# A fused hybrid layer on one core: two tiles that outlive the stages and hold what the next one reads first, a fourth quadrant sum formed with the others, memory keys transposed beside the pair products

## The chip, the core and the metric

One NeuronCore of one Trainium2 chip. The metric is the device time of one execution in microseconds, over several runs. TensorE multiplies matrices into PSUM, VectorE, ScalarE and GpSimd work on tiles in SBUF, and SyncE issues all the DMAs of this kernel in one queue, in program order: an issue that has to wait holds up all that stand behind it.

## What is computed

One layer over two groups of tokens: 1024 prompt tokens, and 8 requests of 16 new tokens each with a cache (128 "sample" tokens). The width is 1024, all numbers are fp32.

```python
u = layer_norm(x)                                   # both groups
q, k, v, g_a, x_r, g_b, q_m, g_c, g_m = split(u @ w_in)       # 1024 -> 11264
# A: differential attention, 8 heads; sample tokens also over cache_k, cache_v (512 past tokens)
o_a = diff_attn(q, k, v, cache) * silu(g_a)
# B: causal convolution of width 4, gated linear recurrence
o_b = rglru(conv(x_r)) * silu(g_b)
# C: attention into 256 memory tokens, 4 heads; sample tokens into cache_mem_k, cache_mem_v
mk, mv = split(mem_prompt @ w_mem_kv)               # mk, mv are outputs too
o_c = softmax(q_m @ mk.T / 16) @ mv * silu(g_c)
m = sum_i sigmoid(g_m[i]) * (o_i @ w_branch[i])
y = layer_norm(alpha * x + m @ w_o)
```

Further outputs are the new keys and values, the last recurrence state and the last rows before the convolution.

## The kernel before

**Products in split form.** TensorE multiplies in a reduced form of fp32 (fp32r). Each operand is split into an upper part, rounded by a ScalarE cast, and a lower part, the rest, by a VectorE subtraction (`split`, L135); `mm3` adds up three products: upper by upper, lower by upper, upper by lower. So the same names come in pairs: `uhi`, `ulo` (the activations, transposed, 1152 tokens), `xh`, `xl` (a weight tile from `xr`).

**Units.** Most of TensorE's work are units (`units_for`, L467): 24 products of 128x384 into a bank named `pj`, for one column tile of weights and one third of the tokens. `m_units` (L500) merges a branch: it loads a gate (`gmr`) and the sum so far (`mr`) from DRAM, adds the gated product and stores the sum (`d_m`). A stage is a `Window`: a list of small functions, `weave`d from its own steps and units that fill TensorE's time. A scheduler then places every instruction by priority, which follows program order but for hoists; tiles and banks carry the waits.

**Stages in order of time** (us of the profiled execution):

- to 196: norms, transposes, memory keys and values (stored in DRAM as `d_kv`), values
- to 683: prompt attention (`window_a`)
- to 720: `window_p` (L1100): `piece` loads quadrants of `u` (k halves by token halves) as `uq` and forms three sums and differences, split into `ut`; units for the merge gates fill
- to some 1335: `window_g` (L1167): the remaining projections in a two-by-two scheme with seven products instead of eight: 28 jobs of seven steps each (`step`, L1336), 24 products of 128x288 per half step into banks `ba`, `bb`, `bc`; the recurrence runs beside them. `start` (L1171) loads the fourth quadrant again (`uz`, ten loads), subtracts and writes the difference over the first part of `uhi`, `ulo`. `g_prep` (L1135) forms sums `s1`, `s2`, `s3` of weight quadrants
- to some 1545: `window_s` (L824): decode attention over the cache: `kload` (L853) brings keys of request b and head group g in two loads of 512 KB, TensorE transposes them (`ktr`), GpSimd puts the queries (`qz<-sq`) and new keys (`kT<-sk`) in place
- to some 1651: `window_c` (L726): memory attention of the prompt. `setup` loads the memory keys, `mk_tr` (L739) transposes them, four steps of four transposes, `qget` and `qput` load and scale and split the queries of a head
- to some 1750: `window_x` (L989): memory attention of the sample tokens, eight requests in turn; `load` (L1007) brings 1 MB of keys and 1 MB of values each; `xq` is the query, scaled by GpSimd from `xqr`
- to the end: the merge of the third branch, the output product, the last norm.

At the end of `window_s` and `window_x`, `swap` (L523) loads the next branch's output (`ocr`, twelve pieces through four buffers) and splits it over `uhi`, `ulo`.

## Time and profile before

| | |
|---|---|
| runs | 1966.18, 1965.82, 1960.79 us |
| median | 1965.82 us |
| profiled execution | 1961.36 us, span 1959.6 us |
| granted TensorE clock, mean | 0.996 |
| busy share TensorE, VectorE, ScalarE, GpSimd | 98%, 64%, 45%, 5% |
| moved by DMA | 296 MB, mean 151 GB/s |
| chain that ended last | TensorE 81%, DMA 8%, VectorE 5%, ScalarE 4% |

The profile shows one execution. Times in its rows count from the start of the span. A row of the timeline is one instruction or several merged ones; the bracket at its end gives how long the engine stood idle before it, and the work of which engine, line or DMA ended that. Products are pipelined: a row's length is longer than the distance to the next row's start, and it is the distance that counts in a series.

### The profile page before, as it was taken

The page shows a single profiled execution, that of the slowest core. Times are in us where ns is not written, and L with a number is a line of the kernel's source. Part 1 is how long each engine was busy: PE and PEld are TensorE (multiplying, and loading weights), DVE is VectorE, ACT ScalarE, POOL GpSimd, SP SyncE. Part 2 cuts the span into 40 slices and gives each one's busy share as a digit, 9 for nine tenths or more (in the row PEclk, how much of TensorE's full clock was granted, in tenths as well). Part 3 has the DMA queues.
Part 4 walks back from the last instruction along what each step waited for, and adds up shares of the span by engine and source line. Part 5 has one row for each costly group of instructions (what it writes and reads, how often), then busy time and mean ns, then how long its engine had stood idle before and what let it go on. Part 6 is the DMA issues. An engine that isn't in the chain of part 4 may idle for free.

```text
span 1959.6 us, 34499 instructions
## 1 busy us (share of the span) xinstructions
PE 1911.8 (98%) x13544; PEld 1811.2 (92%) x13544; DVE 1252.1 (64%) x2536; ACT 891.4 (45%) x1827; POOL 89.1 (5%) x174
## 2 busy tenths in 40 slices
PE   8999999999999999999999999998999999999998
PEld 8999999999999999999999999997788888789986
DVE  7731786677866667767666667664444675464397
ACT  5432565556655543334666666663333442231120
POOL 0000000000000000000000000000110001000000
PEclk9999999999999999999999999999999999999999
DMA  9753122212221174323444444458788875885332
GB/s 300 234 151 104 33 69 81 65 45 66 69 81 37 53 202 132 103 92 105 125 150 128 138 137 136 135 160 264 252 300 259 287 268 191 299 293 178 122 115 87
DMA packets 292114, 296.34 MB, mean 151 GB/s; under 512 B 17572, under 2 KB 249892, under 8 KB 291952
## 3 DMA queue, kind: packets, MB, share of 16 engines
q1 hardware_dynamic: 291952, 294.15, 47.0%
q8 instruction: 106, 1.74, 0.4%
q14 instruction: 56, 0.46, 0.1%
HBM read 209.01 MB, written 85.08 MB: 150 GB/s over the span
## 4 chain that ended last, share of the span: by engine, by line
PE 81%; DMA 8%; DVE 5%; ACT 4%; issue 2%; SPq 1%; DVEq 0%; ACTq 0%
PE pj L140 36%; PE ba L1359 9%; PE bb L1359 9%; PE bc L1359 9%; PE sc L140 5%; PE o L140 4%; PE tr L663 2%; PE tr L879 1%; PE pv L140 1%; PE tr L140 1%; DMA xk<-in_cache_mem_k_dram 1%; DMA ocr<-d_oT 1%; ACT K L589 1%; DVE w L258 1%; PE tr L1020 1%
## 5 line engine op out<-in xcount | busy, mean ns | idle before, releaser
L140 PE MATMUL pj<-uhi,xh 128*128 128x384 f32 x1248 | 428.4, 343 | 1.1 <-DVE gmr L513 1.1
L140 PE MATMUL pj<-uhi,xl 128*128 128x384 f32 x1248 | 421.9, 338 | 0.6 <-DVE xl L133 0.6
L140 PE MATMUL pj<-ulo,xh 128*128 128x384 f32 x1248 | 421.6, 338 | 0.0
L140 PEld LDWEIGHTS pj<-uhi,xh 128*128 128x128 f32 x1248 | 235.2, 188 | 5.4 <-issue 2.7
L140 PEld LDWEIGHTS pj<-uhi,xl 128*128 128x128 f32 x1248 | 234.9, 188 | 2.1 <-DVE xl L133 0.9
L140 PEld LDWEIGHTS pj<-ulo,xh 128*128 128x128 f32 x1248 | 235.3, 189 | 0.8 <-issue 0.4
L136 ACT CAST xh<-xr 128x512 fp32r<-128x512 f32 x143 | 85.5, 619 | 145.1 <-PE pj L140 100.1
L645 ACT ACTIVATE p<-p,sst 128x256 f32<-128x256 f32 (+6 forms) x128 | 100.6, 787 | 17.3 <-DVE sst L642 16.1
L140 PE MATMUL pj<-w,uhi 128*128 128x256 f32 x576 | 105.0, 282 | 0.5 <-ACT uhi L136 0.5
L140 PE MATMUL pj<-wo,mh 128*128 128x512 f32 x432 | 99.2, 390 | 0.6 <-ACT wo L136 0.3
L642 DVE CUSTOM_DVE_ANT_0 p<-sc,th 128x256 f32<-128x256 f32 (+6 forms) x128 | 96.4, 767 | 3.2 <-PE sc L140 2.0
L140 PEld LDWEIGHTS pj<-wo,mh 128*128 128x128 f32 x432 | 80.8, 188 | 18.9 <-ACT wo L136 1.6
L140 PE MATMUL sc<-K,Q 128*128 128x512 f32 (+4 forms) x384 | 94.6, 356 | 0.0
L513 DVE SCALAR_TENSOR_TENSOR gmr<-gmr,pj 128x384 f32<-128x384 f32 x72 | 39.7, 551 | 84.2 <-PE pj L140 61.6
L140 PEld LDWEIGHTS pj<-w,uhi 128*128 128x128 f32 x576 | 89.0, 189 | 1.3 <-ACT uhi L136 1.2
L133 DVE TENSOR_TENSOR xl<-xr,xh 128x512 fp32r<-128x512 f32 x104 | 70.6, 685 | 24.9 <-ACT xh L136 24.5
L140 PE MATMUL pj<-w,ulo 128*128 128x256 f32 x288 | 81.6, 284 | 1.7 <-DVE ulo L133 1.7
L140 PE MATMUL o<-v,wT 128*128 128x128 f32 x576 | 80.2, 278 | 0.0
L140 PEld LDWEIGHTS o<-v,wT 128*128 128x128 f32 x576 | 74.3, 192 | 3.4 <-ACT wT L169 1.5
L573 DVE SCALAR_TENSOR_TENSOR Q<-pj,Q 64x384 fp32r<-64x384 f32 (+1 forms) x48 | 24.5, 511 | 80.7 <-ACT Q L572 80.2
L589 ACT CAST K<-kr 64x384 fp32r<-64x384 f32 (+1 forms) x96 | 45.7, 476 | 48.4 <-DVE kr L584 47.3
L140 PEld LDWEIGHTS sc<-K,Q 128*128 128x128 f32 x384 | 63.9, 189 | 3.8 <-DVE sst L642 1.5
(323 smaller groups left out, 4284.1 us busy)
## 6 DMA issues: line engine op xcount, KB each, us to landing
xr<-in_w_in_dram SPq DMA_DIRECT2D x80, 512.0 KB, 4.0
ck<-in_cache_k_dram SPq DMA_DIRECT2D x32, 512.0 KB, 5.9
cv<-in_cache_v_dram SPq DMA_DIRECT2D x16, 1024.0 KB, 7.7
gmr<-d_gm SPq DMA_DIRECT2D x72, 192.0 KB, 5.2
xr<-in_w_branch_dram SPq DMA_DIRECT2D x24, 512.0 KB, 5.9
d_gm<-go SPq DMA_DIRECT2D x20, 576.0 KB, 3.2
d_m<-gmr SPq DMA_DIRECT2D x48, 192.0 KB, 3.1
mr<-d_m SPq DMA_DIRECT2D x48, 192.0 KB, 2.9
```

What stands on the lines that cost most here:

```text
L133: V.tensor_tensor(out, a, b, OP.subtract)
L136: SC.copy(hi, src)
L140: PE.matmul(out, a, b, start=start, stop=stop)
L258: V.tensor_tensor(l[:, 2 * j:2 * j + 2], src, raw(h[:, 2 * j:2 * j + 2]), OP.subtract)
L513: V.scalar_tensor_tensor(g, g, 1.0, t, op0=OP.add, op1=OP.mult)
L573: V.scalar_tensor_tensor(q[b], t[a, :n], -1.0, raw(q[a]), op0=OP.mult, op1=OP.subtract)
L589: SC.copy(kh[b], kr[a, :n])
L642: V.tensor_tensor_reduce(s[:, :L].rearrange("p (a b) -> p a b", a=nb), ps[z][:, :nb, :w], X["th"][:, 896 - 128 * i:896 - 128 * i + L].rear ...
L645: SC.activation(s[:, :L], s[:, :L], AF.Exp, scale=-1.0, bias=st_[:, z, i:i + 1], accum_out=st_[:, 2 + z, i:i + 1])
L663: PE.transpose(t[:, 128 * j:128 * j + 128], X["w", h, i][:, 128 * k:128 * k + 128], ident)
L879: PE.transpose(t[:, 128 * j:128 * j + 128], X["ck", n, s // 2][:, j, 128 * (s % 2):128 * (s % 2) + 128], ident)
L1359: PE.matmul(t, w[:, p, k, :], m[v][:, k, a], start=first and k == 0 and y == 0, stop=last and k == 3 and y == 2, skip_group_check=True)
```

## The change

- **Fourth quadrant.** `piece` in `window_p` forms the fourth difference from the quadrants that it has loaded anyway, into `uz` (a tile of the new pool `prek`, tag `pk`) and a small rest tile; `start` only splits it. The ten loads and their subtractions in `start` go.
- **Sums of weights.** `s1`, `s2`, `s3` live in a pool (`gs`) that is opened ahead of `window_p`; `g_prep(1)` is called at the end of `window_p`.
- **Two tiles that outlive the stages.** Tag `pk` of `prek` holds in turn `uz`, the first cache keys (`ck0`), the transposed memory keys (`mkr`) and the first keys of `window_x`. Tag `pq` of `preq` holds the first memory query (`qr`), then the first values of `window_x`.
- **Memory keys.** In `window_g`, beside jobs 1 to 5, `mk_get` loads a quarter of the keys and stores it to the output, `mk_tr` transposes it (four transposes), ScalarE copies, and a store takes it to DRAM (`d_mkT`). `c_get` at the end of `window_s` loads all of it, and the first query; `window_c` only splits.
- **Priority.** The last nine attention steps of `window_x` are placed with a priority higher by 100.
- The scratch area for dynamic DMA is set to 1024 bytes.

```diff
@@ window_c
-            mr = wk.tile([128, 2, D], F32, name="mr", tag="Gc")
+            X["qr"] = pre["q"]
             for j in range(4):
...
+                a = slice(2 * j, 2 * j + 2)
+                split(*[z[:, a] for z in X["mkT"]], pre["k"][:, a])
+                if j == 0:
+                    qput(0)
+            pre["xk"] = pre["p"].tile([128, 2, D], F32, name="xk", tag="pk")
+            pre["xv"] = pre["s"].tile([128, 2, D], F32, name="xv", tag="pq")
...
-        at = [lambda j=j: mk_tr(j) for j in range(4)]
+        at = []
         for h in range(MH):
+            if h == 3:
+                at.append(lambda: [SY.dma_start(pre["x" + z], A["cache_mem_" + z][0][0].rearrange(
+                    "(a p) h d -> p a (h d)", p=128)) for z in "kv"])
@@ window_s
+        def first_keys():
+            t = pre["p"].tile([128, 2, 4, 256], F32, name="ck0", tag="pk")
+            for e in range(2):
+                SY.dma_start(t[:, e], ck[0].rearrange("(a p) h d -> p a (h d)", p=128)[:, :, 256 * e:256 * e + 256])
+                X["ck", 0, e] = t[:, e]
...
+        def c_get():
+            pre["k"] = pre["p"].tile([128, 8, 256], F32, name="mkr", tag="pk")
+            SY.dma_start(pre["k"], d_mkT.rearrange("k p t -> p k t"))
+            pre["q"] = pre["s"].tile([128, 2, S], F32, name="qr", tag="pq")
+            SY.dma_start(pre["q"], d_qm[0:2, :, :S].rearrange("d p t -> p d t"))
@@ window_x
+            if b == 0:
+                X["k", 0], X["v", 0] = pre["xk"], pre["xv"]
                 return
...
+        def first(f):
+            with tc.high_priority(100):
+                f()
+        at[n:] = [lambda f=f: first(f) for f in at[n:]]
@@ window_p
+            sub(gp[1][c // 128], q[1, 1], q[0, 1])
@@ window_g
-            gp[0] = wk
-            g_prep(1)
             g_prep(2)
             for c, n in TCS:
-                t = wk.tile([128, 2, 4, 128], F32, name="uz", tag="go", bufs=2)[:, :, :, :n]
-                for k in range(2):
-                    SY.dma_start(t[:, k], d_u[4 * k:4 * k + 4, :, TH + c:TH + c + n].rearrange("k p t -> p k t"))
-                sub(t[:, 1], t[:, 1], t[:, 0])
                 a = (slice(None), slice(0, 4), slice(TH + c, TH + c + n))
-                split(uhi[a], ulo[a], t[:, 1])
+                split(uhi[a], ulo[a], gp[1][c // 128])
...
+        def mk_get(j):
+            c = slice(256 * j, 256 * j + 256)
+            mt_[j] = r = wk.tile([128, 2, 256], F32, name="mk", tag="mk", bufs=2)
+            SY.dma_start(r, d_kv[:, c].rearrange("(a p) d -> p a d", p=128))
+            SY.dma_start(A["out_4"][0, 0].rearrange("(a p) h d -> p a (h d)", p=128)[:, :, c], r)
+
+        def mk_tr(j):
...
+            o = wk.tile([128, 2, 256], F32, name="mo", tag="mo")
+            SC.copy(o, t.rearrange("p (a b) -> p a b", a=2))
+            SY.dma_start(d_mkT[2 * j:2 * j + 2].rearrange("k p t -> p k t"), o)
```

How the instructions stand. SyncE's queue where the memory attention goes over to its decode part (`d_oT` stores of the outputs, `d_m` stores and `gmr`, `mr` loads of the merge, `xqr` the decode query, `xG` its gate), before:

```order
L506 DMA gmr<-d_gm 128x384
L810 DMA d_oT_59<-oc 128x512 x4
L519 DMA d_m<-gmr 128x384
L509 DMA mr<-d_m 128x384
L997 DMA xqr<-d_qm 128x8x128
L1002 DMA xG<-d_gc 128x8x128
L1004 DMA xcs<-in_c_xsel_dram 128x64
L1012 DMA xk<-in_cache_mem_k_dram 128x2x1024
L1012 DMA xv<-in_cache_mem_v_dram 128x2x1024
```

and now:

```order
L805 DMA d_oT_59<-oc 128x512 x3
L520 DMA d_m<-gmr 128x384
L510 DMA mr<-d_m 128x384
L805 DMA d_oT_59<-oc 128x512
L453 DMA xr<-in_w_branch_dram 128x8x128
L507 DMA gmr<-d_gm 128x384
L1007 DMA xqr<-d_qm 128x8x128
L1012 DMA xG<-d_gc 128x8x128
L1014 DMA xcs<-in_c_xsel_dram 128x64
L1025 DMA xk<-in_cache_mem_k_dram 128x2x1024
```

The query stands directly behind a pair of merge transfers before; now a 512 KB weight load (`xr`) and a gate load stand between the last output store and it. The gate load takes a buffer that the store `d_m` ahead of it must have read.

TensorE where the memory attention's first scores (`sc`) are formed, before:

```order
L140 MATMUL pj<-uhi,xl 128x384
L140 MATMUL pj<-uhi,xh 128x384
L140 MATMUL pj<-ulo,xh 128x384
L140 MATMUL pj<-uhi,xl 128x384
L744 MATMUL tr<-ident,mr 128x128 x4
L140 MATMUL sc_17377<-mkT_17186,qm_17360 128x256
L140 MATMUL sc_17377<-mkT_17187,qm_17360 128x256
```

and now:

```order
L140 MATMUL pj<-uhi,xh 128x384
L140 MATMUL pj<-ulo,xh 128x384
L140 MATMUL pj<-uhi,xl 128x384
L140 MATMUL sc_17332<-mkT_17231,qm_17235 128x256
L140 MATMUL sc_17332<-mkT_17232,qm_17235 128x256
L140 MATMUL sc_17332<-mkT_17231,qm_17236 128x256
L140 MATMUL sc_17332<-mkT_17231,qm_17235 128x256
```

The transposes of the memory keys (`mr`) have gone from here. The scores stand behind the 24th product of the merge that is issued in this stage; before, behind the 72nd.

TensorE at the end of the decode part (`tr<-ident,xp` transposes the last probabilities, `pv` multiplies by the values, `o` sums the requests' parts), before:

```order
L140 MATMUL pj<-ulo,xh 128x384
L140 MATMUL pj<-uhi,xl 128x384
L1041 MATMUL tr<-ident,xp 128x128 x2
L140 MATMUL pv<-xv,xpT 32x256 x8
L140 MATMUL o<-xcs,xacc 128x64 x2
L140 MATMUL pj<-uhi,xh 128x384
L140 MATMUL pj<-ulo,xh 128x384
L140 MATMUL pj<-uhi,xl 128x384
```

and now:

```order
L140 MATMUL pj<-ulo,xh 128x384
L140 MATMUL pj<-uhi,xl 128x384
L140 MATMUL pv<-xv,xpT 32x256 x8
L140 MATMUL pj<-uhi,xh 128x384
L140 MATMUL pj<-ulo,xh 128x384
L140 MATMUL pj<-uhi,xl 128x384
L140 MATMUL o<-xcs,xacc 128x64 x2
L140 MATMUL pj<-uhi,xh 128x384
L140 MATMUL pj<-ulo,xh 128x384
```

The value products and outputs followed each other directly; now products of the merge stand between the transposes, the value products and the outputs. Behind the last output 1063 products of 128x384 remain, 1008 before.

## Rows read from the trace of the kernel before

**Rows 1.** The page, busy time by engine (busy us, share of the span, number of instructions):

```profile
PE 1911.8 (98%) x13544; PEld 1811.2 (92%) x13544; DVE 1252.1 (64%) x2536; ACT 891.4 (45%) x1827; POOL 89.1 (5%) x174
```

**Rows 2.** Stretches of the span: its bounds and length in us, busy time of each engine with its number of instructions, granted TensorE clock, mean busy share of the DMA engines, GB/s:

```profile
726.00:746.00 20.00, 15.69 (x109) 14.36 (x108) 13.19 (x24) 7.08 (x15) 0.00 (x0) 1.00 0.64 162
...
1350.00:1365.00 15.00, 10.40 (x56) 7.45 (x55) 2.72 (x4) 2.31 (x4) 2.64 (x10) 0.77 1.05 331
...
1545.00:1552.00 7.00, 4.81 (x30) 4.52 (x29) 2.23 (x4) 0.59 (x1) 0.00 (x0) 1.00 0.93 288
...
1666.00:1730.00 64.00, 62.83 (x512) 50.23 (x510) 29.52 (x73) 17.61 (x40) 0.00 (x0) 1.00 0.81 293
1730.00:1752.00 22.00, 18.26 (x134) 16.13 (x134) 15.82 (x29) 11.54 (x18) 0.00 (x0) 0.95 0.94 299
1752.00:1850.00 98.00, 98.00 (x564) 98.00 (x563) 43.06 (x75) 14.53 (x25) 0.00 (x0) 0.99 0.50 155
```

**Rows 3.** Timeline (start us, length us, engine, line, operation, out<-in, count; in brackets the idle time before it and what ended it), SyncE's queue, start of the product stage, first loads of the fourth quadrant:

```profile
723.11 2.97 SPq L1178 DMA_DIRECT2D uz<-d_u  x4
```

**Rows 4.** Timeline, VectorE, first subtraction of the fourth quadrant:

```profile
727.80 0.69 DVE L133 TENSOR_TENSOR uz<-uz 128x512 f32<-128x512 f32 x1 [1.44 <-DMA uz<-d_u]
```

**Rows 5.** Timeline, TensorE, start of the product stage:

```profile
720.34 0.29 PE L1359 MATMUL ba<-uhi,xl 128*128 128x288 f32 x1
...
735.43 0.40 PE L1359 MATMUL bb<-uhi,xh 128*128 128x288 f32 x1 [1.30 <-ACT uhi L136]
...
741.75 0.40 PE L1359 MATMUL ba<-uhi,xh 128*128 128x288 f32 x1 [1.55 <-DVE go L1374]
```

**Rows 6.** Chain of the work that ended last, in order of time, product stage: a block of 48 products:

```profile
761.81 6.36 PE bc L1359 x48
```

**Rows 7.** Timeline, TensorE, from the product stage into the decode attention:

```profile
1345.06 0.44 PE L140 MATMUL pj<-uhi,xh 128*128 128x384 f32 x1 [1.14 <-DVE gmr L513]
...
1358.27 1.97 PE L879 MATMUL tr<-ident,ck 128*128 128x128 f32 x8 [4.60 <-DMA ck<-in_cache_k_dram]
...
1361.19 1.97 PE L879 MATMUL tr<-ident,ck 128*128 128x128 f32 x8
...
1372.26 1.09 PE L879 MATMUL tr<-ident,ck 128*128 128x128 f32 x8
```

**Rows 8.** Timeline, SyncE's queue, start of the decode attention, load of the query:

```profile
1347.46 0.45 SPq L840 DMA_DIRECT2D sq<-d_qs  x1
```

**Rows 9.** Timeline, GpSimd, start of the decode attention, the query's copies:

```profile
1353.69 1.92 POOL L873 COPY qz<-sq 64x64 f32<-64x64 f32 x4 [63.06 <-PE pj L140]
```

**Rows 10.** Timeline, TensorE, from the decode attention into the memory attention (`mr` are the memory keys):

```profile
1544.42 0.45 PE L140 MATMUL pj<-uhi,xl 128*128 128x384 f32 x1 [0.58 <-DVE xl L133]
...
1548.62 0.63 PE L744 MATMUL tr<-ident,mr 128*128 128x128 f32 x4 [2.19 <-DMA mr<-d_kv]
1549.00 0.43 PE L140 MATMUL pj<-uhi,xh 128*128 128x384 f32 x1
...
1557.08 0.66 PE L744 MATMUL tr<-ident,mr 128*128 128x128 f32 x4 [1.30 <-DVE mkT L133]
```

**Rows 11.** Timeline, ScalarE, start of the memory attention: upper parts of the split keys and of the split query:

```profile
1549.34 0.59 ACT L136 CAST mkT<-tr 128x512 fp32r<-128x512 f32 x1 [6.47 <-PE tr L744]
1553.63 2.02 ACT L765 ACTIVATE qm<-qr 128x1024 fp32r<-128x1024 f32 x2 [3.71 <-DMA qr<-d_qm]
```

**Rows 12.** Timeline, VectorE, the same place: lower part of the split query:

```profile
1554.73 1.23 DVE L766 SCALAR_TENSOR_TENSOR qm<-qr,qm 128x1024 fp32r<-128x1024 f32 x1 [4.01 <-ACT qm L765]
```

**Rows 13.** Timeline, TensorE, from the memory attention into its decode part (`o` the last output, `xk` the keys of the first request):

```profile
1649.53 1.67 PE L140 MATMUL o<-pT,mv 128*128 128x512 f32 x6
1651.03 0.34 PE L140 MATMUL pj<-uhi,xl 128*128 128x384 f32 x1
1651.21 0.34 PE L140 MATMUL pj<-uhi,xh 128*128 128x384 f32 x1
...
1663.63 1.99 PE L1020 MATMUL tr<-ident,xk 128*128 128x128 f32 x16 [1.33 <-DMA xk<-in_cache_mem_k_dram]
1665.54 0.96 PE L140 MATMUL sc<-xkT,xq 128*32 128x256 f32 x6
```

**Rows 14.** Timeline, GpSimd, the same place: the decode query, scaled:

```profile
1658.79 5.62 POOL L1000 TENSOR_SCALAR xq<-xqr 128x1024 f32<-128x1024 f32 x2 [164.29 <-DMA xqr<-d_qm]
```

**Rows 15.** Issues of DMA by line: stores of the merged sum (count, KB of each, median us from issue to landing):

```profile
d_m<-gmr SPq DMA_DIRECT2D x48, 192.0 KB, 3.1
```

**Rows 16.** Timeline, SyncE's queue, load of the decode query:

```profile
1654.37 0.41 SPq L997 DMA_DIRECT2D xqr<-d_qm  x1
```

**Rows 17.** Timeline, TensorE, end of the decode part:

```profile
1747.06 1.07 PE L140 MATMUL pv<-xv,xpT 128*32 128x256 f32 x16 [2.43 <-DVE xpT L1043]
1749.44 1.01 PE L140 MATMUL o<-xcs,xacc 128*128 128x64 f32 x4 [1.31 <-ACT xacc L1052]
...
1751.63 0.52 PE L140 MATMUL pj<-ulo,xh 128*128 128x384 f32 x1
```

**Rows 18.** Timeline, SyncE's queue, end of the decode part: second and last issue of the third branch's output:

```profile
1730.25 0.99 SPq L533 DMA_DIRECT2D ocr<-d_oT  x2
...
1749.60 0.89 SPq L533 DMA_DIRECT2D ocr<-d_oT  x1
```

52 lines of the change are left out of this document (29 added, 23 removed).

## The prediction

> **What bounds the kernel now.** Read the busy shares first: TensorE works for 98% of the span and only some 48 us of 1959.6 are idle [rows 1]. So a term counts only if TensorE waits there, or runs at a lower clock. Next read the stretches [rows 2]: the long middles of the stages are nearly full (98.0 of 98 us, 62.8 of 64), the holes lie in short stretches at the stage boundaries: 15.7 of 20 us where the pair products begin, 10.4 of 15 at a granted clock of 0.77 where the decode attention begins, 4.8 of 7 at the memory attention, 18.3 of 22 at the end of its decode part. The change works at just these places and at the start of that decode part. Then the timelines tell which wait ends last at each.
>
> The sum is made against the profiled execution, 1961.36 us (span 1959.6, 1.8 around it). It lies 4.5 below the median shown, 1965.82, and within the three runs.
>
> **1. Pairs to products (quadrant difference).** Removed: ten loads of the fourth quadrant and five subtractions at the start of the product stage. The loads are issued from 723.1 on [rows 3], and VectorE waits for the first until 727.8 [rows 4]. TensorE starts at 720.34 and waits, among others, 1.30 and 1.55 us for results behind them [rows 5]. By 741.75 it has issued 120 products; an undisturbed block of 48 takes 6.36 us [rows 6], so 120 need 15.9 of the 21.4 that passed: 5.5 lost. The idle time of the stretch bounds it from below (4.3, [rows 2]); from above I put 6.1, as some of the idle follows later in the stretch. Added: five subtractions of 0.69 in the earlier stage, where VectorE is far from full and the tiles are loaded anyway. The splits of the difference stay, but their source is in SBUF; ScalarE and VectorE need some 4 us for them, while TensorE first has 48 other products (6.4 us). **I take 5.5 (4.3 to 6.1).** If the cover were gone, the splits would be late by 1 to 2.
>
> **2. Products to decode attention (first cache keys).** Now: 1.14 idle, then 4.60 for the keys, then eight transposes in 1.97 us that take 1.09 later [rows 7]. The half clock lasts from 1358.3 to about 1364.5, so it costs half of 6.2, 3.1 us. Together 8.8. The keys are now resident since the products began, and TensorE goes straight on through their transposes. What is late next is the decode query: its issue stays near 1347.5 [rows 8], since the queue ahead of it keeps its stores and loads; GpSimd starts on it when it has landed, at 1353.7, and is through with it at 1355.6 [rows 9]. By the changed order TensorE stands at the first score at about 1351.8. New wait: 3.8. The gain is 8.8 - 3.8 = 5.0, or 1.9 if the clock halves again as after the 4.60. A wait of 2.19 left the clock at 1.00 [rows 2, 10], one of 4.60 did not; 3.8 lies between, so I charge half of the 3.1. **I take 3.5 (1.9 to 5.0).** The 1 MB load of the first memory query that now goes ahead in this queue is counted: it is issued while the queue waits anyway.
>
> **3. Decode to memory attention (keys transposed beforehand, first query loaded).** Now: 0.58, 2.19 (for the keys) and 1.30 idle, 4.1 in sum [rows 10]; and ScalarE can start on the query, loaded after the keys, only at 1553.6 [rows 11]. The sixteen transposes move into the product stage: four of them delay the next product by 0.38 us (1548.62 to 1549.00, [rows 10]), so sixteen cost 1.5 there and give 1.5 back here. ScalarE's four copies and the 2 MB of extra stores and loads per kernel lie beside full TensorE stages; free. After: the scores follow directly on the first unit, 48 products of the merge earlier in the order. They need one split of the keys and two of the query, 0.6 and two times about 1.0 on ScalarE [rows 11] with 1.2 each on VectorE behind them [rows 12]; both engines get to them while TensorE is still in its first unit, so they are ready 0 to 1.5 us after TensorE gets there. **I take 3.0 (2.0 to 4.1).**
>
> **4. Memory attention to its decode part (first keys and values loaded early).** Here I expect a loss. Now: after the last output matmul, which ends at 1651.2, 64 products and sixteen transposes follow, with 1.33 idle for the keys; the first score is at 1665.54, 14.3 later [rows 13]. GpSimd's scaled query is done at 1664.4 [rows 14], so it is hidden behind the keys by about a microsecond. After: the transposes come at once, then 39 products at 0.175 us [rows 13], and TensorE stands at the first score 8.8 us after the last output. But the query's load is not moved forward; in the new queue order a 512 KB weight load and a gate load stand before it, and that gate load waits until a store has landed (3.1 us, [rows 15]). The store is issued about 0.3 after the last output, so the query goes out at about 3.5 (now 3.2, [rows 16]), lands 4.4 later as now, and takes GpSimd 5.6 [rows 14]: first score at 13.5, a wait of 4.7. At that score 24 more products are left than now, 4.2 us. Loss: 13.5 + 4.2 - 14.3 = 3.4, and half of the 3.1 for the clock, as above. **I take -5.0 (-7 to -3).**
>
> **5. End of the decode part (last nine steps at higher priority).** Now: 2.43 and 1.31 idle in the last chain, then products that last 0.52 us where they last 0.34 elsewhere [rows 17, 13]. The granted clock is 0.95 over those 22 us and 0.99 over the 98 that follow [rows 2], that is 1.1 and 1.0 lost to it; 5.8 in sum with the idle. After: products stand between the last transposes, the value products and the outputs, and 55 more products follow the last output. The steps of the last two requests are packed closer before that, at 3 products between them; such steps wait for copies of 0.2 to 1 us, so 1.7 is charged. **I take 4.0 (2.0 to 5.8).**
>
> The smaller scratch area issues nothing and costs nothing.
>
> Sum: 5.5 + 3.5 + 3.0 - 5.0 + 4.0 = 11.0, so 1961.4 - 11.0 = **1950.4**. Ends: gains of 4.3 + 1.9 + 2.0 - 7 + 2.0 = 3.2 and 6.1 + 5.0 + 4.1 - 3 + 5.8 = 18.0, that is 1943.4 to 1958.2.
>
> **The rivals.** *A: the query of the decode part is in time.* If the queue reaches it before the last outputs, as its operands would allow, part 4 becomes a gain of 1.3 (today's idle) and no clock is lost; with the other parts at their upper ends the gain is 6.1 + 5.0 + 4.1 + 1.3 + 5.8 = 22.3: 1939.1. Against it: the order of the queue is fixed and the wait for the store stands ahead. 0.10.
>
> *B: the branch output loads at the end are the bound.* Twelve loads bring the third branch's output through four buffers, each buffer freed by a split. Now their issues run from 1730.3 to 1750.5, 20 us [rows 18], and the last split follows some microseconds later. In the new order three to four units of 24 products (12.5 to 16.7 us) cover them. The loads now stand among the last attention loads, so they will be quicker alone; if they are not, TensorE waits 8 instead of gaining 4, and a gain of 11 becomes about -1: 1962. Decides: the last piece over 16.7 us after the first load. 0.12.
>
> *C, slower: the clock falls over and over in the decode part.* This stage alternates short attention pieces with products. By the two orders the change takes 55 of about 290 products out of it, so each of its eight requests has some 29 where 36 stood, 1.2 us less cover for the chain of copies, softmax and GpSimd. TensorE is idle for only 1.2 us in 64 there now [rows 2]. If each of seven requests waits long enough to be followed by half clock, at 3.1 each, the stage loses 21.7: 1972. It decides when the added wait per request comes near the 4.60 that halved the clock at the decode attention; 1.2 us less cover is far from that. 0.05. The Trainium skill ("TensorE: Matmul & The Clock Gate", section "HAM oscillation — how this bites in real kernels") describes this: a kernel that waits for a transfer at every tile falls to the lower clock at every tile and pays each time. By that rule the time would be C's. The trace agrees with the single step of it (0.77 after 4.60 idle), but shows no repeated fall in this stage, where the clock is 1.00.
>
> *D: the loads moved were never last* (the query at 2 and 4 lands later than reckoned and takes the whole gain there). Then parts 2 and 4 give 0 and -8 and the sum is 4.5: 1957. 0.12.
>
> **How the numbers follow.** Forecast 0.61, A 0.10, B 0.12, C 0.05, D 0.12. The range takes in the forecast's own (1943.4 to 1958.2) and reaches up towards B, since the runs of before lie up to 4.8 above the profiled one: 1942 to 1960. About 0.3% (5.9 us) is what a measurement can tell from no change; against the median of 1965.8, faster means below 1959.9. Forecast, A and D lie there nearly always (0.77 of 0.83), B and the rest of D are the same (0.17), C is slower, with a little of B (0.06).
>
> **What would show it.** Right: no load of the quadrant between 720 and 740 and TensorE's first job 22.5 long; the transposes of the first cache keys with no wait, and a wait of 3 to 5 us at the first score, released by GpSimd; the same, 4 to 6 us, at the first score of the decode part; products between the last value products and the outputs. Wrong: a wait for a transfer in the middle of the product stage (the new key transposes or their store standing in the queue), or a clock below 1.00 over more than 10 us of any stage, or the decode part's end waiting for the branch output.

## The result

| | before | after |
|---|---|---|
| median (runs) | 1963.3 us (4) | 1950.75 us (4) |
| lowest to highest | 1960.62 to 1966.18 | 1949.24 to 1953.19 |
| profiled execution, span | 1961.36, 1959.6 | 1949.6, 1947.8 |
| granted TensorE clock, mean | 0.996 | 0.996 |

The ratio is 0.9943 [0.9929, 0.9958]: 12.5 us less by the medians, 11.8 by the profiled executions; 11.0 was forecast. A second series of the same kernel, with its own runs of before, gave 1949.52 (1946.74 to 1952.00), 0.9946 [0.9932, 0.9960]; it is called the repeat below.

Where the time came from is read off TensorE's timeline at five marks: the first product of the product stage, its last, the transposes of the decode attention's output (eight, `tr<-ident,sob`), the last output of the prompt's memory attention, the end of the span.

| between the marks, us | before | after | repeat | forecast change |
|---|---|---|---|---|
| product stage | 615.24 | 611.55 | 611.57 | -4.0 (5.5 less 1.5 for the key transposes) |
| decode attention | 183.97 | 178.74 | 178.81 | -3.5 |
| memory attention, prompt | 131.65 | 130.40 | 129.72 | -4.5 (3.0, and the 1.5 back) |
| its decode part, to the end | 308.40 | 305.87 | 309.50 | +1.0 (5.0 less 4.0) |
| sum | 1239.26 | 1226.56 | 1229.60 | -11.0 |

At the fourth mark the same number of products is left in both (one record differs), so the last stretches hold the same work. The stage before the first mark is 0.9 longer after. The last stretch of one and the same code differs by 3.6 us between two profiles; no term under that size can be read there from one profile. The two stages before it spread as much, though the two columns hide it: over all profiles below whose code in the stage is that of after, the decode attention took 178.7 to 182.6 (ten profiles) and the prompt's memory attention 129.7 to 134.7 (five); the product stage, where it is unedited, 611.5 to 612.4.

### The profile page after: what moved, and what is told of

It is laid out like the page before. It is cut to its first block, busy times and chain, and to the rows that moved or that the text cites. A ratio compares the mean times of both kernels' runs of the same rounds, so it can differ in the third digit from the quotient of the medians.

```text
span 1947.8 us, 34510 instructions
## 1 busy us (share of the span) xinstructions
PE 1907.1 (98%) x13544; PEld 1810.6 (93%) x13544; DVE 1250.7 (64%) x2536; ACT 892.9 (46%) x1831; POOL 88.0 (5%) x174
## 4 chain that ended last, share of the span: by engine, by line
PE 86%; DVE 5%; DMA 4%; ACT 4%; issue 2%; SPq 0%; POOL 0%; POOLq 0%; DVEq 0%; ACTq 0%
PE pj L140 39%; PE ba L1372 9%; PE bc L1372 9%; PE bb L1372 9%; PE sc L140 6%; PE o L140 5%; PE tr L666 2%; PE pv L140 1%; PE tr L883 1%; PE tr L140 1%; ACT K L592 1%; DVE xcv L1240 1%; PE tr L1033 1%; DMA wor<-in_w_o_dram 1%; DMA wr<-in_w_mem_kv_dram 1%
## 5 line engine op out<-in xcount | busy, mean ns | idle before, releaser
L648 ACT ACTIVATE p<-p,sst 128x256 f32<-128x256 f32 (+6 forms) x128 | 100.6, 787 | 17.3 <-DVE sst L645 16.7
```

What stands on the lines that cost most here:

```text
L648: SC.activation(s[:, :L], s[:, :L], AF.Exp, scale=-1.0, bias=st_[:, z, i:i + 1], accum_out=st_[:, 2 + z, i:i + 1])
```

## The profile after

The page's busy times by engine, as [rows 1]: TensorE has the same instructions, 4.7 us less busy time, and 7 us less idle time.

```profile
PE 1907.1 (98%) x13544; PEld 1810.6 (93%) x13544; DVE 1250.7 (64%) x2536; ACT 892.9 (46%) x1831; POOL 88.0 (5%) x174
```

Stretches of the kernel after (bounds and length, busy time and instructions of each engine, granted clock, DMA share, GB/s), to be held against [rows 2]:

```profile
726.00:746.00 20.00, 20.00 (x153) 20.00 (x152) 11.74 (x20) 6.39 (x15) 1.18 (x4) 1.00 0.46 141
1345.00:1360.00 15.00, 12.86 (x80) 9.86 (x79) 4.02 (x9) 2.34 (x5) 2.85 (x16) 1.00 1.00 303
...
1550.00:1565.00 15.00, 12.64 (x65) 11.51 (x65) 9.31 (x14) 7.03 (x16) 0.00 (x0) 0.89 0.93 321
...
1658.00:1664.00 6.00, 6.00 (x36) 4.88 (x29) 2.06 (x5) 0.56 (x2) 0.00 (x0) 0.65 0.79 311
1664.00:1720.00 56.00, 55.85 (x487) 45.89 (x487) 26.91 (x66) 15.74 (x36) 0.00 (x0) 1.00 0.76 264
1720.00:1745.00 25.00, 25.00 (x172) 23.03 (x172) 16.86 (x30) 12.66 (x21) 0.00 (x0) 1.00 0.89 279
```

The start of the products and the end of the decode part have lost their holes: 20.0 of 20 busy, 25.0 of 25. The decode attention has smaller ones, 12.9 of 15 busy where 10.4 stood, and a clock of 1.00 where 0.77 stood. But two stretches have a lower clock that were undisturbed before: 0.89 inside the prompt's memory attention (in the repeat 1.00 over the same 15 us), 0.65 at the first score of the decode part.

The chain of work in order of time, product stage: two blocks of the second and third job of the kernel after, one job apart.

```profile
756.67 6.37 PE bc L1372 x48
...
779.79 6.37 PE bb L1372 x48
```

A job is seven steps of 24 products, 12 per half step. From the first product to the first of these blocks, 264 products (a job of 168 and 96 of the next), it takes 756.67 - 721.24 = 35.43; before, for as many, 761.81 - 720.34 = 41.47 [rows 5, 6]. The first job alone is 22.3 long: its 169th product is issued at 743.50. The 168 products from block to block take 779.79 - 756.67 = 23.12; before, that distance ended with this row of the chain,

```profile
784.36 6.36 PE bb L1359 x48
```

that is 784.36 - 761.81 = 22.55. The 0.57 between go with the four key transposes that now stand there, and a wait of 0.19 behind them.

TensorE's timeline after, at the places of [rows 5, 7, 10, 13, 17] (start, length, what; in brackets the idle time before it and what ended it):

```profile
721.24 0.29 PE L1372 MATMUL ba<-uhi,xl 128*128 128x288 f32 x1
...
1343.96 0.44 PE L140 MATMUL pj<-uhi,xh 128*128 128x384 f32 x1 [1.06 <-DVE gmr L514]
1350.62 0.63 PE L140 MATMUL sc<-kT,qz 128*32 128x264 f32 x2 [1.16 <-POOL qz L877]
...
1366.23 0.64 PE L140 MATMUL sc<-kT,qz 128*32 128x264 f32 x4 [1.16 <-ACT kT L170]
...
1538.79 0.97 PE L140 MATMUL sc<-mkT,qm 128*128 128x256 f32 x5
1558.40 0.50 PE L140 MATMUL o<-pT,mv 128*128 128x512 f32 x1 [2.34 <-ACT pT L136]
...
1640.28 1.65 PE L140 MATMUL o<-pT,mv 128*128 128x512 f32 x6 [0.27 <-DVE oc L804]
1657.61 1.93 PE L140 MATMUL sc<-xkT,xq 128*32 128x256 f32 x16 [7.14 <-POOL xq L1010]
...
1728.70 1.07 PE L140 MATMUL pv<-xv,xpT 128*32 128x256 f32 x16
1729.70 0.44 PE L140 MATMUL pj<-uhi,xh 128*128 128x384 f32 x1
1730.33 0.65 PE L140 MATMUL o<-xcs,xacc 128*128 128x64 f32 x4
```

The first score of the memory attention before, to be held against the row at 1538.79:

```profile
1560.19 2.04 PE L140 MATMUL sc<-mkT,qm 128*128 128x256 f32 x15
```

SyncE's queue after, as [rows 8, 16, 18]: the decode attention's query; the decode query; first and last load of the branch output.

```profile
1345.53 0.43 SPq L837 DMA_DIRECT2D sq<-d_qs  x1
...
1644.52 0.67 SPq L1007 DMA_DIRECT2D xqr<-d_qm  x1
...
1710.68 0.95 SPq L534 DMA_DIRECT2D ocr<-d_oT  x2
...
1739.15 2.23 SPq L534 DMA_DIRECT2D ocr<-d_oT  x2
```

GpSimd's timeline after, as [rows 9, 14]:

```profile
1350.05 1.08 POOL L877 COPY qz<-sq 64x64 f32<-64x64 f32 x4 [62.20 <-DMA sq<-d_qs]
...
1651.95 5.60 POOL L1010 TENSOR_SCALAR xq<-xqr 128x1024 f32<-128x1024 f32 x2 [165.49 <-DMA xG<-d_gc]
```

The wait of 7.14 at the first score of the decode part ends with these two: the query is issued at 1644.52, GpSimd starts 7.4 later and works for 5.6. The row names the gate's load (`xG`), issued right behind the query, as what came last; in the repeat it names the query's own. GpSimd's step reads the query alone. And ScalarE's timeline after, at the first output of the memory attention: it stands 4.53 us for the next head's values, and the copy of the probabilities (`pT`), for which TensorE then waits 2.34, comes behind them in its order.

```profile
1552.50 0.62 ACT L136 CAST mv<-mvr 128x512 fp32r<-128x512 f32 x1 [4.53 <-DMA mvr<-d_kv]
...
1557.75 0.60 ACT L136 CAST pT<-tr 128x512 fp32r<-128x512 f32 x1
```

## The experiments

Unless said otherwise an edit is made on the kernel after. "Decode part" is the last row of the table above, from the last output of the prompt's memory attention to the end: 305.87 and 309.50 for the unedited kernel.

**The unedited kernel again, for the spread.**

> The changed kernel once more, unedited, beside the two that follow: how far its stages spread from one profile to the next. Expected: 1949 to 1953 us; the product stage within 0.3 us of 611.6, the decode part with the rest behind it between 305.9 and 309.6 (the values that runs with the same code there have shown). If the spread is much smaller, the differences of 2 to 3 us between the single parts undone are real; if not, only the larger ones are.

Measured: 1949.52, ratio 0.9946. In its profile the wait at the first score of the decode part is 6.09 (7.14 in the first); and 2.56 us of another wait stand in the middle of that part. TensorE, then the stretch around the second:

```profile
1655.21 1.94 PE L140 MATMUL sc<-xkT,xq 128*32 128x256 f32 x16 [6.09 <-POOL xq L1010]
...
1701.84 0.93 PE L1033 MATMUL tr<-ident,xk 128*128 128x128 f32 x4 [2.56 <-DVE xkT L172]
```

```profile
1700.00:1710.00 10.00, 8.16 (x60) 5.74 (x61) 4.16 (x8) 0.37 (x1) 0.00 (x0) 0.83 0.64 232
```

What follows: the new wait for GpSimd is there each time (5.6 to 7.1 in all seven profiles of kernels that load the keys early and the query late); the other one does not stand in the first profile, whose timeline has no wait of that size between its first score and 1720. It costs 2.56 and some 1.7 of clock (0.17 of 10 us); less the 1.05 by which the wait for GpSimd is shorter, that is 3.2 of the 3.6 by which the two profiles differ.

**Part 1 undone: the quadrant loaded again.**

```diff
@@ piece
-            sub(gp[1][c // 128], q[1, 1], q[0, 1])
@@ start
+                t = wk.tile([128, 2, 4, 128], F32, name="uz", tag="go", bufs=2)[:, :, :, :n]
+                for k in range(2):
+                    SY.dma_start(t[:, k], d_u[4 * k:4 * k + 4, :, TH + c:TH + c + n].rearrange("k p t -> p k t"))
+                sub(t[:, 1], t[:, 1], t[:, 0])
...
-                split(uhi[a], ulo[a], gp[1][c // 128])
+                split(uhi[a], ulo[a], t[:, 1])
```

> The changed kernel with the fourth quadrant loaded again and subtracted at the start of the product stage, as before; all else stays. Theory (TensorE lost 5.5 to 6.1 us there behind these loads): 5.5 to 6.1 us more than the changed kernel, about 1956.5, and the waits of 1.3 and 1.5 us at the start of the stage come back. Rival (the sums of weights and their pool were late, not the quadrant): 0 to 1.5 us more.

Measured: 1962.07, ratio 0.9998 [0.9987, 1.0009]; the whole gain is gone. The product stage takes 621.64, which is 10.1 longer than after. Its TensorE waits and the stretches around them:

```profile
730.56 3.48 PE L1375 MATMUL ba<-ut,xl 128*128 128x288 f32 x24 [1.86 <-ACT gx L1382]
...
737.54 0.61 PE L1375 MATMUL bb<-uhi,xh 128*128 128x288 f32 x1 [2.62 <-ACT uhi L136]
```

```profile
730.00:740.00 10.00, 6.70 (x40) 6.14 (x41) 7.19 (x12) 4.30 (x10) 0.00 (x0) 0.85 0.80 224
740.00:750.00 10.00, 9.51 (x48) 8.97 (x47) 2.60 (x6) 2.55 (x7) 0.00 (x0) 0.63 0.63 189
```

What follows: removing the reload is needed for the gain, but 10.1, more than was expected, is not the worth of part 1 by itself. The two waits are 4.5 of it, the lower clock some 5.2 (0.15 and 0.37 of 10 us each), where 1.00 stood before [rows 2]. In this kernel the new loads of the memory keys stand between the quadrant's; that they are the reason for the higher cost is likely but was not tried by itself. The kernel before against after gives 6.04 for the first 264 products.

**Part 2 undone: first cache keys loaded in the stage.**

```diff
-            if 0 < n < 16:
+            if n < 16:
...
-        wk.seq += [lambda: pre["ck"](), lambda: [b_get(z, 0) for z in range(6)], ...
+        wk.seq += [lambda: [b_get(z, 0) for z in range(6)], ...
```

> The changed kernel with the first cache keys loaded inside the decode attention, as before. Theory (4.6 us wait for the keys, and half clock behind it): 5.2 us more than the changed kernel, about 1956, and the decode query lands 1.5 to 2 us later because four key loads stand near it. Rival (the decode query is what is late in either case): 1 to 2 us more.

Measured: 1956.69, ratio 0.9968 [0.9958, 0.9978], 4 to 5 us slower than the kernel after by the ratios. TensorE's timeline:

```profile
1343.55 0.44 PE L140 MATMUL pj<-uhi,xh 128*128 128x384 f32 x1 [3.06 <-DVE gmr L514]
1355.14 1.09 PE L883 MATMUL tr<-ident,ck 128*128 128x128 f32 x8 [1.43 <-DMA ck<-in_cache_k_dram]
...
1564.49 0.79 PE L140 MATMUL o<-pT,mv 128*128 128x512 f32 x1 [5.55 <-ACT pT L136]
```

What follows: by the ratios part 2 is worth 4 to 5; the interval just touches that of after (0.9958) and overlaps that of the repeat (up to 0.9960). The stage is 4.0 longer than after (182.71), but the ten profiles with the keys early reach 182.6, so the stage alone does not show it. In this profile the loss sits in the wait for the merge's gate (3.06 instead of 1.06) more than in that for the keys (1.43); that the gate is late because of the keys' loads beside it is likely but was not tried by itself. The prompt's memory attention, whose code is unedited, is 4.3 longer too (134.69), by the same wait for `pT` as in the kernel after, here 5.55.

**Part 3 undone: memory keys transposed in place.**

```diff
@@ setup
+            mr = wk.tile([128, 2, D], F32, name="mr", tag="Gc")
...
+                SY.dma_start(mr[:, :, c], d_kv[:, c].rearrange("(a p) d -> p a d", p=128))
...
@@ window_c
+        at = [lambda j=j: mk_tr(j) for j in range(4)]
...
@@ window_g
-                wk.seq.append(lambda j=i - 1: mk_get(j))
...
-                wk.seq.append(lambda j=i - 2: mk_tr(j))
```

> The changed kernel with the memory keys transposed at the start of the prompt's memory attention, and the first query loaded there, as before. Theory (each part of the change pays by itself): waits of 4.1 us and 1.5 us of transposes come back there, 2.3 us of transposes go from the product stage: 3 to 3.5 us more than the changed kernel, about 1954. Rival (what the stage wins at its start it loses later by the wait for probabilities of 2.34 us and the half clock behind it, which go with the early start): 0 to 1 us less, about 1950.

Measured: 1953.82, ratio 0.9960 [0.9946, 0.9974]; against the kernel after the medians differ by about 3 to 4 us, but the intervals of the ratios overlap (from 0.9946 here, up to 0.9958 and 0.9960 there). The stages give both signs of the forecast term: the product stage 1.4 shorter (610.16), the prompt's memory attention 4.2 longer (134.58). TensorE's timeline, first memory keys:

```profile
1539.01 0.63 PE L749 MATMUL tr<-ident,mr 128*128 128x128 f32 x4 [2.42 <-DMA mr<-d_kv]
```

What follows: part 3 is worth about 3 by the medians, not clear of the spread, and the transposes' price in the product stage is 1.4. The wait for the keys themselves is back, 2.42 (2.19 in [rows 10]). The 4.2 are not the price of the transposes' place alone: the stage is also 2.9 longer than in the kernel before, whose code there is nearly the same, with a wait of 2.75 for `oc`, the output's copy.

**Part 4 undone: keys and values of the decode part loaded in it.**

```diff
-            pre["xk"] = pre["p"].tile([128, 2, D], F32, name="xk", tag="pk")
-            pre["xv"] = pre["s"].tile([128, 2, D], F32, name="xv", tag="pq")
...
-            if b == 0:
-                X["k", 0], X["v", 0] = pre["xk"], pre["xv"]
-                return
```

> The changed kernel with the first keys and values of the decode part of the memory attention loaded inside that part, as before; all else stays. Theory (the early keys only exposed the wait for GpSimd's query, which then cost a half clock, and their 2 MB stand in the way in the prompt part): the 7.1 us wait and the 2.34 us wait in the prompt part go, a wait of about 1.3 for the keys comes back, 3 to 7 us less than the changed kernel, about 1944 to 1948. Rival (the early loads relieve the decode part's own transfers, and what the first score loses is won back by the later requests): 0 to 4 us more, 1951 to 1955.

Measured: 1947.83, ratio 0.9934 [0.9918, 0.9949]. The decode part takes 302.86, which is 3.0 and 6.6 shorter than in the two profiles of the unedited kernel. The first score comes as late as with part 4 (15.71 after the last output; 15.68 with it, 14.62 in the repeat), but with 31 products of 128x384 fewer still to do, 5.4 us at 0.175 [rows 13]. TensorE, keys of the first request:

```profile
1657.98 2.04 PE L1025 MATMUL tr<-ident,xk 128*128 128x128 f32 x16 [1.58 <-DMA xk<-in_cache_mem_k_dram]
```

What follows: the sign of the forecast loss is borne out in the profiles: all six whose decode part is that of after, part 5 included, took 305.9 to 309.6. The ratio alone (0.9934 against 0.9943 and 0.9946) does not settle it. The wait for `pT` in the prompt's part, which was expected to go, is still there, 2.57: the early keys and values are not its cause.

**Part 4 completed: the query loaded and scaled early.** The decode query is loaded and scaled beside the second head, the first keys beside the fourth; the values go back to their old place.

```diff
+        def xq_get():
+            q = pre["p"].tile([128, 8, 128], F32, name="xqr", tag="pk")
+            SY.dma_start(q, d_qm.rearrange("h p t -> p h t")[:, :, S:T])
+            pre["xq"] = pre["s"].tile([128, 8, NB, 2, NS], F32, name="xq", tag="pq")
...
+            if h == 1:
+                at.append(xq_get)
...
+            X["q"] = pre["xq"]
```

> The changed kernel, but the tile that outlives the stages holds the scaled query of the decode part of the memory attention instead of the first request's values: the query is loaded in the prompt part, beside its second head, and scaled there by GpSimd; the first values are loaded in the decode part like all others. Theory (the wait for GpSimd's query is what the early keys ran into): the 7.1 us idle at the first score of the decode part goes, and the half clock behind it (2.1), unless the next request's keys are then late by 2 to 3; 6 to 9 us less than the changed kernel, about 1941 to 1944. Rival (the decode part is bound by its loads, so that the wait only moves to the keys of the second request): 0 to 2 us less, 1949 to 1951.

Measured: 1950.59, ratio 0.9940 [0.9924, 0.9956], no faster than the kernel after. The decode part is shorter, 301.62; its first score comes 3.95 after the last output, without a wait. But the prompt's part takes 133.58, 3.2 to 3.9 more than in the two profiles of the unedited kernel. TensorE's timeline:

```profile
1572.31 2.93 PE L140 MATMUL o<-pT,mv 128*128 128x512 f32 x6 [4.14 <-DVE oc L802]
...
1649.33 0.63 PE L140 MATMUL sc<-xkT,xq 128*32 128x256 f32 x6
```

SyncE's queue ahead of the wait of 4.14:

```profile
1559.90 0.46 SPq L752 DMA_DIRECT2D qr<-d_qm  x1
...
1562.16 0.45 SPq L803 DMA_DIRECT2D d_oT<-oc  x1
```

VectorE at its end:

```profile
1571.56 0.69 DVE L802 SCALAR_TENSOR_TENSOR oc<-o,Gc 128x512 f32<-128x512 f32 x1 [6.12 <-DMA d_oT<-oc]
```

What follows: the missing query was the cause of the wait in the decode part. With it taken away there, a wait stands in the stage before: TensorE waits for `oc`, the output's copy. The copies have two buffers, so VectorE's copy at 1571.56 needs the store issued at 1562.16, and by the trace's records of landings that store lands only at 1571.47. Ahead of it in the queue stands the 1 MB load of the next head's query (`qr`, 1559.90), which lands at 1567.66. That the early query put this wait there rests on single profiles: the prompt's part takes 133.3 to 134.5 in all four kernels with the query early, but 134.7 also in the one with the cache keys late, where the query is not early. The wait for `pT` is not there in this kernel, and ScalarE does not stand still for the next head's split.

**Is it the split of the values?** ScalarE's order puts the next head's values ahead of `pT`. The edit moves the text of that split behind the two score steps.

```diff
-            split(hl[0], hl[1], mr)
+            X["mvr", h] = mr
...
+            at += [..., lambda h=h: s1(h, 1), lambda h=h: split(*X["mv", h], X["mvr", h]), ...
```

> The changed kernel with one edit in the prompt's memory attention: the split of a head's memory values is written behind the head's two groups of scores instead of ahead of them. Theory (ScalarE stands still for 4.5 us ahead of the second group's exponentials because the split of the next values waits for their load, and the wait of 2.34 us on TensorE with the half clock behind it follows from that): that wait goes, 2.3 to 4 us less than the changed kernel, about 1947 to 1948.5. Rival (the exponentials wait for something else, or the queue's order moves with the edit): within 1 us of the changed kernel.

Measured: 1951.54, ratio 0.9948 [0.9934, 0.9963], no change. ScalarE's timeline:

```profile
1551.21 0.62 ACT L136 CAST mv<-mvr 128x512 fp32r<-128x512 f32 x1 [4.71 <-DMA mvr<-d_kv]
1551.73 0.47 ACT L785 ACTIVATE p<-sc,mz 128x256 f32<-128x256 f32 x1
```

TensorE waits 1.83 for `pT`. What follows: nothing on the cause, since the scheduler places the split ahead of the probabilities all the same, and ScalarE stands there for 4.71.

**Both edits together** (the query early, and the text of the split moved):

> Both edits together: the decode query loaded and scaled in the prompt part instead of the first values held, and the split of the memory values behind the scores. The first alone came out level with the changed kernel: the wait for GpSimd was gone, but the prompt part lost 4.1 us in a new wait behind output stores that the crowded queue issued late. Theory (the crowding comes from loads that the waiting splits hold up): that wait goes with the second edit, 6 to 9 us less than the changed kernel, about 1942 to 1945. Rival (the queue of loads sets the pace of the two parts together, whatever waits last): within 2 us of the changed kernel.

Measured: 1948.5, ratio 0.9935 [0.9923, 0.9948]. Decode part 300.39, prompt part 133.96 with waits of 3.59 for `pT` and 1.45 for `oc`. As with the query alone, a gain in the one stage goes with a loss in the other.

**The long holds taken later.** Query and keys both go beside the fourth head, into tiles that are free by then; the fourth head's own query takes the tile `pq`.

```diff
+            if h == 3:
+                X["qr"] = r = pre["s"].tile([128, 2, S], F32, name="qr", tag="pq")
...
+                at.append(xq_get)
+                at.append(xk_get)
```

> The changed kernel with other tenants of the two tiles: the scaled decode query takes the tile of the memory keys, the fourth head's query and then the first request's keys take the other, so that the keys load only when that query is used up, some 45 us later than now; the first values load in the decode part. Theory (the decode part gains 5 to 6 us when query and keys are both there, and the prompt part loses 3 to 4 us only because 2 MB are loaded in its first 20 us): the prompt part stays at 130 to 131 us, the decode part with the rest is at 300 to 302; 4 to 6 us less than the changed kernel, about 1945 to 1947. Rival (whatever waits last in the prompt part, the two parts together are paced by their loads): within 2 us of the kernel that holds the query early, 1948 to 1951.

Measured: 1946.51 (1944.77 to 1949.77), ratio 0.9929 [0.9915, 0.9943]. Decode part 298.97, the prompt's part still 134.48. ScalarE, then SyncE, then TensorE:

```profile
1558.28 0.62 ACT L136 CAST mv<-mvr 128x512 fp32r<-128x512 f32 x1 [7.45 <-DMA mvr<-d_kv]
```

```profile
1547.31 2.96 SPq L510 DMA_DIRECT2D mr<-d_m  x2
1554.91 0.32 SPq L507 DMA_DIRECT2D gmr<-d_gm  x1
1555.28 0.43 SPq L744 DMA_DIRECT2D mvr<-d_kv  x1
```

```profile
1564.18 0.80 PE L140 MATMUL o<-pT,mv 128*128 128x512 f32 x1 [5.25 <-ACT pT L136]
```

The lower ratio is not clear of that of after: the intervals overlap (up to 0.9943 here, from 0.9929 there). What follows: the early holds were not the cause of the wait in the prompt's part, which was expected at 130 to 131. The chain there is: the queue issues nothing from 1550.3 to 1554.9, ahead of a gate load (its buffer has to be stored first); the values' load stands behind that gate; ScalarE stands for the values; `pT` stands behind them. The store that holds the gate load up was issued at 1545.56 and lands at 1554.90, behind a 1 MB query load that lands at 1554.37; stores of this kind took 3.1 in the median before [rows 15].

**The same, with one buffer for the split values**, so that the split cannot go ahead of the outputs that read the old ones:

```diff
-            hl = [wk.tile([128, 2, 256], F32R, name=f"mv{z}", tag=f"mv{z}", bufs=2) for z in range(2)]
+            hl = [wk.tile([128, 2, 256], F32R, name=f"mv{z}", tag=f"mv{z}") for z in range(2)]
```

> The kernel with the later tenants of the two tiles (scaled query, fourth head's query, first keys), and the split memory values of a head in one buffer instead of two, so that the next head's split can't stand on ScalarE ahead of this head's exponentials; the loads of the values keep two buffers. Theory (the wait for probabilities at the first output of the prompt part, 1.7 to 5.6 us from profile to profile, and the half clock behind it come from ScalarE, which is in order and stands still 3.9 to 7.5 us in front of that split until its load has landed): the wait goes, the prompt part takes 127 to 129 us, and with the decode part kept at 299 to 301 the kernel takes about 1942 to 1945. Rival (the queue of loads sets the pace there: the store ahead of the load holds everything that follows): the wait moves to the next output, the part stays at 130 us or more, 1946 to 1949.

Measured: 1945.61 (1943.44 to 1947.06), ratio 0.9914 [0.9899, 0.9929]: the lowest median here, faster than before by 17 us and than the kernel after by 4 to 6 (by medians and by ratios; the intervals of the ratios touch at 0.9929 only). TensorE, then SyncE:

```profile
1570.19 2.93 PE L140 MATMUL o<-pT,mv 128*128 128x512 f32 x6 [3.38 <-DVE oc L805]
```

```profile
1556.57 1.43 SPq L755 DMA_DIRECT2D qr<-d_qm  x1
...
1560.76 0.32 SPq L806 DMA_DIRECT2D d_oT<-oc  x1
```

What follows: the wait for `pT` at this place is gone, so the split ahead of it was its cause. The other profiles bear this out: in all seven whose split is unedited and held up (after, repeat, quadrant reloaded, cache keys late, no priority, keys of the decode part late, holds late), the wait for `pT` is ScalarE's idle time before the split less 2.2 (3.87 and 1.68, 4.53 and 2.34, up to 7.74 and 5.55); in the four where ScalarE does not stand idle there (before, priority alone, keys in place, query early) there is none. But the stage hardly gets shorter by it. A wait of 3.38 for `oc` takes its place, as in the kernel with the query early and in the same way: the store issued at 1560.76, whose buffer the copy needs, lands at 1569.35, behind a query load of 1 MB issued at 1556.57 that lands at 1567.70. The prompt's part (133.28) gains only about a microsecond on the one with both holds late (134.48). The 3.6 us between the two profiles lie in the decode attention (182.6 and 178.8), whose code is the same in both, so what the one buffer is worth by itself is not shown. Moving the query's load behind the stores was not tried.

**Part 5 undone.**

```diff
-        at[n:] = [lambda f=f: first(f) for f in at[n:]]
```

> The changed kernel without the higher priority of the last nine attention steps of the decode part. Theory (the last chain of the attention stood bare and half clock followed): idle of 3.7 us and 2.0 us of half clock come back at the end of that part, 4.0 to 5.8 us more than the changed kernel, about 1955 to 1957. Rival (the end became bare only because the loads of the branch output shared the time, and the earlier keys of the first request have moved these apart): 0 to 2 us more.

Measured: 1954.3, ratio 0.9960 [0.9945, 0.9974], about 3 slower than the kernel after, with overlapping intervals. The last output of the decode part comes 100.31 after the mark; with the priority at 89.05 (92.90 in the repeat), and 57 more products, 9.9 us at 0.174, are then still to do. The decode part as a whole takes 308.01, inside the 305.87 to 309.50 of the unedited kernel. Of what was expected to come back there, the idle time did (21.8 of 25 us busy from 1735 on), the lower clock did not: it is 1.00 there. TensorE at that output:

```profile
1743.73 0.66 PE L140 MATMUL o<-xcs,xacc 128*128 128x64 f32 x4 [2.42 <-ACT xacc L1065]
```

**Part 5 alone**, on the kernel before:

```diff
+        def first(f):
+            with tc.high_priority(100):
+                f()
+        at[n:] = [lambda f=f: first(f) for f in at[n:]]
```

> The kernel before with one thing added: the higher priority of the last nine attention steps of the decode part. Theory (the bare end of the attention chain and the half clock behind it were lost time): 4.0 to 5.8 us less than the kernel before. Rival (the steps packed closer wait for their transfers, which come no earlier): 0 to 2 us less.

Measured: 1955.47, ratio 0.9975 [0.9964, 0.9985], that is 4.9 us (2.9 to 7.1) less than before. The decode part is 304.23 instead of 308.40. Stretches: the start of the products, whose code is that of before, and the time after the last output:

```profile
726.00:746.00 20.00, 17.02 (x109) 15.53 (x108) 13.51 (x24) 7.25 (x15) 0.00 (x0) 0.91 0.61 151
...
1740.00:1840.00 100.00, 100.00 (x578) 100.00 (x578) 48.73 (x83) 21.53 (x35) 0.00 (x0) 1.00 0.59 184
```

What follows from the two: alone the priority is worth 4 to 5, and it does what was reckoned: no idle time at the end of the part (25.0 of 25 us busy from 1715 to 1740; 3.74 idle in [rows 17]) and a clock of 1.00 over 100 us behind it, where 0.95 and 0.99 stood [rows 2]. Undone in the changed kernel it costs about 3, which is not clear of the spread.

## Why the prediction was right

The forecast (1950.4, 11.0 less) held: 1950.75, 11.8 less in the profile. The five terms did not all hold, and their misses cancelled: by the table above the memory attention gained 3.25 less than forecast, the cache keys 1.7 more and the decode part 3.5 more. That the sum came within a microsecond is in part luck.

- **1, quadrant, 5.5: right.** The first 264 products take 6.04 less, at the upper bound of 6.1. VectorE and ScalarE form and split the difference in time: the stretch after is full.
- **2, cache keys, 3.5: mechanism right, the new wait sized too large.** The new wait at the first score, released by GpSimd, is there, but 1.16 instead of 3.8. The query is issued at 1345.53 and GpSimd starts 4.5 later, where I took 6.2 from [rows 8, 9], and its four copies took 1.08 instead of 1.92; no lower clock followed. Two waits of 0.86 and 1.16 for the copies of the transposed keys came in. The stage gained 5.2 in these two profiles, 1.4 to 5.2 over the ten; by the ratios undoing the part costs 4 to 5.
- **3, memory keys: the failed term.** The first scores come 13.38 earlier after the mark (27.26 instead of 40.64), of which 48 products moved behind them are 8.33; the 5.05 left agrees with 3.0 and the 1.5 of the transposes. The transposes cost 4 x 0.57 = 2.3 in the product stage by the jobs, 1.4 by the experiment; 1.5 was forecast. But the stage as a whole gained 1.25 instead of 4.5. I stopped the reckoning at the first scores. What failed is that the copies behind them would keep pace: `pT` waits behind the next head's split, which waits for a load that the queue holds back, and TensorE waits 2.34 and runs at 0.89 over 15 us. These 2.34 and 1.7 are more than the 3.25 that are missing. The experiments show that chain: the wait is ScalarE's idle time less 2.2 in seven profiles, and without that idle time there is none at this place. Ahead of it stands a load: the store at 1542.53 lands at 1548.53, behind the next head's query of 1 MB (1548.02), the gate load waits for that store, and the values' load is issued behind the gate's, at 1548.91. Taking the wait away made the stage hardly shorter (133.28 against 134.48), as a wait for `oc`, whose store landed late behind a query load, took its place.
- **4, decode part, -5.0: right in sign and place, too small.** The first score is 1.34 later than before and has 24 more products behind it, 4.17: 5.5 lost against 3.4 forecast. A granted clock of 0.65 over 6 us followed, 2.1 more where 1.55 was charged; the 7.6 lie past the -7 that I gave as the end. The wait is 7.14, forecast 4.7: the queue came to the query 2.6 after the last output (I said 3.5), but GpSimd could start only 7.4 after the issue (I said 4.4; 6.4 in the repeat). That is the term that was mis-sized: the weight load and the gate load ahead of the query were reckoned as two more issues, and their transfers at nothing. By the trace's records they land in the order of issue, the weight load of 512 KB at 1649.16, the gate's at 1649.73, the query at 1651.54. In all seven profiles with these two ahead of the query it is used 6.4 to 7.4 after its issue, in the three without (before, priority alone, keys in place) 4.4 to 4.7. The experiments with the query early show the cause: no wait, and 4 to 11 us off the decode part, of which 1 to 4 remain against the kernel with neither keys nor query early (302.86).
- **5, priority, 4.0: right.** 4.2 in the stage and 4.9 by the ratio when done alone. Two readings behind it were off. The 1.0 charged for the clock behind the stage came from a rounded 0.99: the clock of before is 0.87 over 1752 to 1756 and 1.00 from there to 1850, that is 0.5. And 432 of the products counted behind the last output are the output product's, of 128x512; of 128x384 there are 633, and 576 before.

Of the 2.5 by which the last stretch is shorter (against +1.0 forecast), the pieces between first score and last output took 73.37 us for 192 products, before 84.91 for 225: 33 products are 5.7, 5.8 remain, more than the priority alone gave. In the repeat 0.9 remain, and the whole stretch is 1.1 longer than before, as forecast; in the two other profiles with the same code of this part (quadrant reloaded, cache keys late) 3.0 and 5.5 remain. So this gain moves from profile to profile, and what makes it was not traced.

**The rivals.** A did not happen in the changed kernel; made to happen, its gain in the decode part is real (first score at 3.95), and the prompt's part takes 3 to 4 of it. B: what was to decide it came out as B's, since the loads of the branch output go out over 28.5 us (1710.68 to 1739.15), more than 16.7; but TensorE does not wait for them, and the end is full. They start 18 us ahead of the last value products (1728.70). C: the clock is 1.00 over 1664 to 1720, after one fall behind the 7.14. By the Trainium skill ("TensorE: Matmul & The Clock Gate", section "HAM oscillation — how this bites in real kernels") a kernel that waits at each tile pays for the lower clock at each. The trace shows the single step (0.65) and no repetition, as there is no long wait at the later requests; in the repeat there is one such wait and one more fall (2.56, 0.83). D: at place 2 the query came earlier than reckoned, and undoing parts 2 and 3 costs 4 to 5 and about 3. At place 4 it came later, and the loss of 7.6 is near D's 8; the time is not D's because the rest of that stretch gained.

**The signs named ahead.** No load of the quadrant, the first job 22.3 long, no wait at the transposes of the cache keys, and products between the last value products and the outputs: these came as said. The waits at the two first scores did not have the size: 1.16 for 3 to 5, and 7.14 (6.09) for 4 to 6. Of the signs against the forecast one came in part, a clock of 0.89 over 15 us in the memory attention; the repeat does not show it.

**The argument on the clock fell.** I took it that a wait of 2.19 leaves the clock at 1.00 and one of 4.60 does not, and charged half between. Waits of 2.34 and 2.56 were followed by 0.89 and 0.83, in other places 2.43 and 1.31 by 0.95 [rows 2, 17], while the 2.42 at the same place without the priority left it at 1.00.

## What to carry to other kernels

Where an operand is loaded early, ask for every other operand of the same instruction: part 4 brought the keys forward, the query became last, and the work that had covered it stood behind the wait. Follow a moved step beyond its first instruction, to the next in-order engine that stands for a load: a gain at the first score was given back at the first output. Undo each part of a mixed change by itself; here the two versions with query and first keys of the decode part early and their tiles held late had the lowest medians, at ratios of 0.9929 and 0.9914 against 0.9943; only the second is clear of the kernel after. And before a difference of one stage is read as the worth of an edit, look how far that stage moves in profiles whose code there is the same: here by 4 to 5 us, as much as most of the terms. A load put ahead of another in one queue costs the other not an issue but a transfer: the query landed behind a weight load of 512 KB, and stores behind query loads of 1 MB.

## What was not expected of the hardware

- The time from issue to use of the same load is not fixed: the decode query `xqr` was used 4.4 us after its issue before [rows 14, 16], 7.4 after, 6.4 in the repeat and 4.7 with the memory keys in place; `sq` 6.2 before [rows 8, 9] and 4.5 after. For `xqr` it goes with what stands ahead of it in the queue.
- Loads and stores of the one queue land in the order of issue: from the decode attention on, all but seven of some 380 in a profile do by the trace's records. A store issued at 1545.56 lands at 1554.90 behind a load of 1 MB, where the median of its kind is 3.1 [rows 15]. So a large load goes with late stores behind it, and a buffer that such a store reads stays taken.
- One wait's length does not tell the clock that follows. The same code in 726 to 746 shows a granted clock of 1.00 in one profile [rows 2] and 0.91 in that of the priority alone.
- GpSimd's four copies of 64x64 took 1.92 in one profile and 1.08 in the other: two of the four were 0.6 to 0.7 long where the rest took 0.23.
- The same reload of the quadrant cost the first 264 products 6.0 us in the kernel before, and the stage 10.1 where loads of the memory keys stood between its own; the cause was not tried by itself.
